# NSA's z gates and its selection and window values computed in the Strassen phase, kept in DRAM by rows, and read back by the attention; finer steps of its background work

## The chip, the cores and the metric

One core of one Trainium2 chip runs the whole kernel in one launch. The metric is the device time of one execution in microseconds (us); lower is better. The engines are named as the profile names them: PE (TensorE's matmuls), PEld (its weight loads), DVE (VectorE), ACT (ScalarE), POOL (GpSimd) and SP (SyncE, which here only issues DMAs).

## The reference, cut to what matters

One hybrid decoder layer on 512 tokens of width 2048, all in float32. FoX is an attention with a forget gate, NSA one with three branches (compressed, selected, window); each has 8 heads of 128.

```python
h = x @ w_in                       # 2048 -> 11808 columns, cut into the groups below
(fq, fk, fv, ff, fz, nq, nkc, nvc, nks, nvs, nkw, nvw, ng, nz, ga, gb) = split(h)
y_a = (fox(fq, fk, fv, ff) * silu(fz)) @ w_a
y_b = (nsa(nq, K and V of each branch, gates(ng)) * silu(nz)) @ w_b
merged = sigmoid(ga) * y_a + sigmoid(gb) * y_b
out = layer_norm(2 ** 0.25 * x + merged @ w_o)
```

The change concerns `nz` (1024 columns, one block of 128 for each NSA head) and `nvs` and `nvw` (256 columns each, one block of 128 for each of the two groups of four heads).

## The kernel before, in words

Every product is made of three matmuls (`mm3`, L105): both operands are split into a high part of 32-bit "r" type and the remainder, and high x high, high x low and low x high are summed in PSUM. A split (`split`, L96 on ACT for the high part, L97 on DVE for the low part) precedes every use of a weight or of an intermediate result.

The weights come as a stream of units. `stream` walks the list `units`; before unit n it emits the split of unit n + 3 (`AHEAD`), whose raw weights SP has loaded before. The order of every engine's instructions is the order in which this Python code emits them; nothing reorders them afterwards.

There are two ways to make columns of `h`:

- A dense projection (`proj`, `dense`) makes 128 columns for all 512 tokens, transposed: [128 columns, 512 tokens]. It has 16 tiles of the contraction with 3 matmuls of 128x512 each, in 4 units, and ends with `evac`.
- The phase of seven products (`pairs`, called by `phase_split`) makes two blocks of `width` columns by Strassen's scheme, with tokens, contraction and columns each cut in two: 7 products x 8 tiles x 2 token tiles x 3 = 336 matmuls of 128x`width` instead of 384. Some of its operands are sums of weights, made on DVE and by accumulating DMAs that POOL issues. Its results lie by rows (tokens on partitions); `keep` stores them in DRAM. Before, it makes FoX's v (L1108 into `v_d`) and most of the two merge gates (`sig_d`): three jobs of width 512 and two of width 384.

The phases follow each other: two first projections and some small ones, the phase of seven products, FoX's heads, NSA's heads, the remaining merge gates (four dense projections of 128 columns, `evac_sig`), then the output products with `w_a`, `w_b`, `w_o`, and the layer norm.

The attention itself is background work: Python generators which `tick` advances by one step. `dense` calls `tick` after every second of its tiles, so 8 times per projection. The queue `sq` runs the score half of one head at a time (`nsa_s`: scores into two banks "s" of PSUM, then in the next step the DVE instruction of L397 that adds the bias and finds the minimum, and ACT's exp of L399; a step later DVE's reciprocal and normalization, L404 and L406). The queue `tq` runs the value half (`nsa_t`: PE transposes of the probabilities, L417, into two banks "pt"; in the next step the split into `pT` on ACT and DVE; two steps later the product with the values). One call of `tick` emits, in this order, a step of every job in `active`, a step of the value half and a step of the score half. `drain` calls `tick` without matmuls of a projection in between, until a condition holds.

In the NSA phase before, the order of the projections is q0 z0, K and V of group 0 (ks, kw, vs, vw), q1 z1 q2 z2 q3 z3, K and V of group 1, q4 z4 ... q7 z7, and then the four gate tiles. `nsa_open`, ahead of the first ks, drains FoX's attention; `o_open`, ahead of the last gate tile, drains NSA's. `evac_z` (L294, L295) applies the gate function to a projection; `evac_v` copies V, transposes it on PE (L357) and splits it.

Of the kernel before, what the change touches and what calls it, by code (L numbers as in the profile page):

```python
# [20 lines left out]
P = 128  # L21
# [42 lines left out]
def layer(ctx, tc, x, w_in, b_f, pos_k, pos_v, wk1, wk2, wv1, wv2, w_a, w_b, w_o, ln_g, ln_b, rel, onehot, out):  # L64
    nc = tc.nc

    def dram(t, off, ap):
        return bass.AP(tensor=t.tensor, offset=t.offset + off, ap=ap)
# [21 lines left out]
    def bank(tag, bufs):  # L90
        return ps.tile([P, S], F32, name=tag, tag=tag, bufs=bufs)

    def split(hi, lo, src, scale=None):

        if scale is None:
            nc.scalar.activation(hi, src, AF.Copy)  # L96
            nc.vector.tensor_tensor(lo, src, hi.bitcast(F32), op=ALU.subtract)  # L97
        else:
            nc.scalar.activation(hi, src, AF.Copy, scale=scale)
            nc.vector.scalar_tensor_tensor(lo, src, scale, hi.bitcast(F32), op0=ALU.mult, op1=ALU.subtract)  # L100
# [35 lines left out]
    def drain(cond):  # L136
        for _ in range(5000):
            if cond():
                return
            tick()  # L140
        raise AssertionError("the background work stands still")
# [70 lines left out]
                u["pre"] = pre  # L212
            units.append(u)

    def dense(w, ncols, col, rows, get_src, evac, pre=None, each=None):

        kts = rows // P
        st = {}

        def pe(u, k0):  # L220
            if k0 == 0:
                st["ps"] = bank("d", 2)
            hi, lo = (t.rearrange("p (k c) -> p k c", c=P) for t in u["w"])
            for k in range(4):
                if each:
                    each(k0 + k)
                mm3(st["ps"], (hi[:, k], lo[:, k]), get_src(k0 + k), k0 + k == 0, k0 + k == kts - 1)
                if k % 2 == 1:
                    tick()
            if k0 + 4 == kts:  # L230
                evac(st["ps"])

        for k0 in range(0, kts, 8):
            add_chunk(lambda r: r.rearrange("p (k c) -> p k c", c=P),
                      dram(w, k0 * P * ncols + col, [[ncols, P], [P * ncols, 8], [1, P]]),
                      lambda u, half, k0=k0: pe(u, k0 + 4 * half), pre=pre if k0 == 0 else None)
# [4 lines left out]
    def proj(col, evac, **kw):  # L241
        dense(w_in, IN_COLS, col, D, x_src, evac, **kw)
# [12 lines left out]
    def pool(name):  # L255
        return stage[name][1]
# [9 lines left out]
    def take(tag):  # L266

        drain(lambda: free[tag] > 0)
        free[tag] -= 1

    def take_later(tag):
        while free[tag] == 0:
            yield
        free[tag] -= 1
# [4 lines left out]
    def z_tile():  # L279
        return pool("hd").tile([P, S], F32, name="z", tag="z", bufs=5)  # L280
# [8 lines left out]
    def evac_z(key):  # L289
        def f(p):  # L290
            take("z")

            zt[key] = t = z_tile()
            nc.scalar.activation(t, p, AF.Tanh, scale=0.5)  # L294
            nc.vector.scalar_tensor_tensor(t, t, 1.0, p, op0=ALU.add, op1=ALU.mult)  # L295
            done.add(("z", key))
        return f
# [16 lines left out]
    def v_load(h):  # L314
# [11 lines left out]
        split(hi, lo, v)  # L326
        done.add(("v", ("f", h)))

    def evac_q(key):
        def f(p):  # L330
            take("q")
            t = pool("attn").tile([P, 2, S], F32R, name="q", tag="q", bufs=2)
            split(t[:, 0], t[:, 1], p, SC)
            qt[key] = t
            done.add(("q", key))
        return f

    def evac_k(key, dst):
        def f(p):
            hi, lo = dst()  # L340
            split(hi, lo, p)
            done.add(("k", key))
        return f

    def evac_v(key, dst):

        def f(p):
            take("vT")
            v = pool("attn").tile([P, S], F32, name="vT", tag="vT", bufs=1)
            nc.scalar.activation(v, p, AF.Copy)  # L350

            def job():
                yield
                yield
                m = bank("m", 1)
                for j in range(NT):
                    nc.tensor.transpose(m[:, j * P:(j + 1) * P], v[:, j * P:(j + 1) * P], ident)  # L357
                free["vT"] += 1
                hi, lo = dst()
                split(hi, lo, m)  # L360
                done.add(("v", key))
                yield
            active.append(job())
        return f


# [8 lines left out]
    def wait_for(*keys):  # L375
        while not all(k in done for k in keys):
            yield
# [236 lines left out]
    zd = [dp.tile([P, S], F32, name=f"z_d{h}") for h in range(NZD)]  # L614
    rawd = {(kv, g): dp.tile([P, S], F32, name=f"raw_d{kv}{g}") for kv in "kv" for g in range(G)}
    vd = dp.tile([S, H * DH], F32, name="v_d")
    sigd = [dp.tile([S, D], F32, name=f"sig_d{g}") for g in range(2)]

    def tables():
# [274 lines left out]
    def nsa_k_dst(br, g):  # L894
        def f():
            if br == "s":
                drain(lambda: all(("s", ("n", h)) in done for h in range(g * HPG)))
                t = pool("nsa").tile([P, 2, KW], F32R, name="nk", tag="nk", bufs=1)
                kt_[g] = t
                nc.vector.tensor_copy(t[:, :, :CP], kt_["c", g].bitcast(F32))  # L900
            t = kt_[g]
            c0 = CP if br == "s" else CP + S
            return t[:, 0, c0:c0 + S], t[:, 1, c0:c0 + S]
        return f

    def nsa_v_dst(br, g):
        def f():
            assert all(("t", ("n", h)) in done for h in range(g * HPG)), "values still held"
            t = pool("nsa").tile([P, 2, NT, DH], F32R, name="nv" + br, tag="nv" + br, bufs=1)
            vt[br, g] = (t[:, 0], t[:, 1])  # L910
            return t[:, 0].rearrange("p j d -> p (j d)"), t[:, 1].rearrange("p j d -> p (j d)")
        return f

    def nsa_kv(g):
        def vpre():
            drain(lambda: all(("t", ("n", h)) in done for h in range(g * HPG)))
        proj(C_KS + g * DH, evac_k(("s", g), nsa_k_dst("s", g)), pre=None if g else nsa_open)
        proj(C_KW + g * DH, evac_k(("w", g), nsa_k_dst("w", g)))
        proj(C_VS + g * DH, evac_v(("s", g), nsa_v_dst("s", g)), pre=vpre if g else None)
        proj(C_VW + g * DH, evac_v(("w", g), nsa_v_dst("w", g)))  # L920


    HT = 2
# [159 lines left out]
    def t_op(n):  # L1083
        if n in ("T4", "T1"):
            return lambda e, k, i: left[n][:, e, k, i * P:(i + 1) * P]
        return lambda e, k, i: left[n, k // 2][:, e, k % 2, i * P:(i + 1) * P]
# [24 lines left out]
    def kept(dst, func, base_col, cols, width):  # L1111
        f = keep(dst, func)
        f.base = base_col
        return (w_in, IN_COLS, 0, [base_col + c for c in cols], width, f)
# [3 lines left out]
    def phase_split():  # L1118
        jobs = [kept(vd, AF.Copy, C_FV, (0, S), S)]
        for g, c in enumerate((C_GA, C_GB)):  # L1120
            jobs.append(kept(sigd[g], AF.Sigmoid, c, (0, S), S))
            jobs.append(kept(sigd[g], AF.Sigmoid, c, (2 * S, 2 * S + W2), W2))
        ops = {n: t_op(n) for n in ("T1", "T2", "T3", "T4")}
        ops.update({"B11": b_op(0, 0), "B21": b_op(1, 0), "B22": b_op(1, 1)})
        pairs(jobs, ops, KT // 2, pairs_open)
# [30 lines left out]
    for kv, h in (("v", 4), ("k", 1)):  # L1156
        for n, l0 in enumerate(range(0, CMP_LEN, 2 * LB)):
            units[at[h] + 4 * n + 4:at[h] + 4 * n + 4] = cmp_units(kv, l0)
    for h in range(H):
        if h % HPG == 0 and h:  # L1160
            nsa_kv(h // HPG)
        proj(C_NQ + h * DH, evac_q(("n", h)))
        proj(C_NZ + h * DH, evac_z(("n", h)))
        if h == 0:
            nsa_kv(0)


    sig, osp, fin = {}, {}, {}

    def evac_sig(g, j):  # L1170

        def f(p):
            take("z")
            t = z_tile()
            nc.scalar.activation(t, p, AF.Sigmoid)

            def job():
                yield
                yield
                m = bank("s", 2)  # L1180
                for i in range(NT):
                    nc.tensor.transpose(m[:, i * P:(i + 1) * P], t[:, i * P:(i + 1) * P], ident)
                nc.scalar.activation(t, m, AF.Copy)
                nc.sync.dma_start(dram(sigd[g][:], j * P, [[D, P], [P * D, NT], [1, P]]),
                                  t.rearrange("p (i c) -> p i c", i=NT))
                free["z"] += 1
                yield
            active.append(job())
        return f
# [12 lines left out]
                    yield  # L1202
        active.append(job())

    for j in range(NG // P, KT):
        for g, c in enumerate((C_GA, C_GB)):
            proj(c + j * P, evac_sig(g, j), pre=o_open if (j, g) == (KT - 1, 1) else None)

    BANKS = [("pt", 2), ("pt", 2), ("o", 1), ("m", 1)], [("d", 2), ("d", 2), ("s", 2), ("s", 2)]

# [351 lines left out]
```

## Time and profile before

| what | us |
|---|---|
| median of 3 runs | 1523.29 (1522.69 to 1524.36) |
| the profiled execution's own time | 1525.12 |
| its span, first to last instruction | 1523.4 |
| PE busy | 1504.0 (99% of the span) |
| DVE busy | 836.7 (55%) |
| ACT busy | 647.0 (42%) |
| phase of seven products | from 106 to about 467 |
| FoX's heads | from about 467 to 755 |
| NSA's heads and the remaining gates | from 755 to about 1156 |

The granted clock was 0.999 of the full 2.4 GHz. A PE that is busy is not one at its peak: the duration of a matmul in the trace holds its latency too, and consecutive ones overlap. The time that a matmul costs is the distance between the starts of neighbours.

### The profile page before, as it was taken

To read this page: it belongs to the slowest core of one execution; us is meant where nothing else is said; L and a number is where in the kernel's file an instruction comes from. 1 tells how busy PE (TensorE), PEld (TensorE's weight loads), DVE (VectorE), ACT (ScalarE), POOL (GpSimd) and SP (SyncE) were. 2 spreads that over 40 slices of the span, in tenths; PEclk is the share of its full clock that TensorE was granted. 3 is DMA by queue.
4 is the path that set the end of the run, shared out by engine and by line. 5 is a ranking of instruction groups with operands and counts; after the bars stand their busy time and mean duration, and the time that the engine had idled before them with its cause. 6 is when DMAs were issued, how large, how long until landed. Compare 5 with 4: busy or idle time off the path is not lost.

```text
span 1523.4 us, 19742 instructions
## 1 busy us (share of the span) xinstructions
PE 1504.0 (99%) x7161; PEld 1256.0 (82%) x7161; DVE 836.7 (55%) x1680; ACT 647.0 (42%) x1270; POOL 210.6 (14%) x351
## 2 busy tenths in 40 slices
PE   8999999999999999999999999999999999999998
PEld 6688788987998888888888888888888888888886
DVE  4566666666664654654435665366645444444455
ACT  6255656555563543533334444244444222222233
POOL 1211010111114623422000000000002010030001
PEclk9999999999999999999999999999999999999999
DMA  8678585877666443443233222322236343272236
GB/s 227 156 220 183 183 194 161 197 214 180 161 161 190 144 136 91 144 138 108 72 98 90 75 77 73 87 76 77 56 96 209 125 145 125 91 249 97 97 111 166
DMA packets 202929, 208.59 MB, mean 137 GB/s; under 512 B 12768, under 2 KB 153104, under 8 KB 202832
## 3 DMA queue, kind: packets, MB, share of 16 engines
q1 hardware_dynamic: 181936, 158.88, 34.9%
q0 software_dynamic: 20608, 47.93, 14.2%
q8 instruction: 56, 0.92, 0.2%
q10 hardware_dynamic: 288, 0.52, 0.1%
q14 instruction: 41, 0.34, 0.1%
HBM read 190.72 MB, written 20.22 MB: 138 GB/s over the span
## 4 chain that ended last, share of the span: by engine, by line
PE 92%; DVE 4%; ACT 2%; DMA 1%; issue 1%; POOL 0%; SPq 0%; ACTq 0%; DVEq 0%; POOLq 0%
PE d L105 50%; PE s L105 13%; PE pt L105 9%; PE o L105 9%; PE m L105 6%; DVE wl L97 2%; PE pt L417 2%; ACT wh L96 1%; PE m L111 1%; PE o L111 0%; PE d L1234 0%; DMA sig_d<-zo 0%; DVE c L993 0%; DVE s L992 0%; DMA vT<-v_d 0%
## 5 line engine op out<-in xcount | busy, mean ns | idle before, releaser
L105 PE MATMUL d<-big,wh 128*128 128x512 f32 x1792 | 568.7, 398 | 1.4 <-ACT wh L96 1.1
L97 DVE TENSOR_TENSOR wl<-wr,wh 128x512 fp32r<-128x512 f32 (+1 forms) x492 | 331.5, 682 | 379.1 <-ACT wh L96 368.7
L96 ACT ACTIVATE wh<-wr 128x512 fp32r<-128x512 f32 (+1 forms) x492 | 299.8, 618 | 388.5 <-PE d L105 140.0
L105 PEld LDWEIGHTS d<-big,wh 128*128 128x128 f32 x1792 | 324.1, 188 | 65.2 <-issue 2.1
L105 PE MATMUL d<-big,wl 128*128 128x512 f32 x896 | 351.5, 392 | 0.1
L105 PEld LDWEIGHTS d<-big,wl 128*128 128x128 f32 x896 | 168.5, 188 | 37.9 <-DVE wl L97 0.9
L399 ACT ACTIVATE p<-p,mn 128x128 f32<-128x128 f32 (+3 forms) x96 | 54.0, 562 | 133.5 <-DVE mn L397 133.5
L97 DVE TENSOR_TENSOR wl<-s,wh 128x512 fp32r<-128x512 f32 (+1 forms) x120 | 75.2, 637 | 54.1 <-ACT wh L96 53.9
L96 ACT ACTIVATE wh<-s 128x512 fp32r<-128x512 f32 (+1 forms) x120 | 69.0, 587 | 58.3 <-DVE wl L97 32.8
L105 PE MATMUL s<-wh,T 128*128 128x512 f32 (+1 forms) x320 | 93.2, 367 | 0.0
L105 PE MATMUL o<-wh,big 128*128 128x512 f32 (+1 forms) x224 | 84.3, 376 | 2.6 <-ACT wh L96 2.6
L105 PE MATMUL m<-wh,big 128*128 128x512 f32 (+1 forms) x224 | 83.7, 374 | 0.0
L105 PE MATMUL d<-wh,big 128*128 128x512 f32 (+1 forms) x240 | 74.4, 376 | 0.0
L97 DVE TENSOR_TENSOR pT<-pt,pT 128x512 fp32r<-128x512 f32 (+1 forms) x96 | 46.6, 488 | 44.3 <-ACT pT L96 43.9
L105 PEld LDWEIGHTS s<-wh,T 128*128 128x128 f32 x320 | 59.2, 188 | 7.5
L805 POOL TENSOR_SCALAR af<-raw,posT 128x31 f32<-128x31 f32 x128 | 65.2, 531 | 0.1
L96 ACT ACTIVATE pT<-pt 128x512 fp32r<-128x512 f32 (+1 forms) x96 | 41.2, 433 | 46.8 <-PE pt L417 46.0
L105 PE MATMUL s<-wl,T 128*128 128x512 f32 (+1 forms) x160 | 58.7, 367 | 0.0
L105 PEld LDWEIGHTS o<-wh,big 128*128 128x128 f32 x224 | 42.0, 188 | 10.6 <-ACT wh L96 4.5
L105 PEld LDWEIGHTS d<-wh,big 128*128 128x128 f32 x240 | 44.7, 188 | 7.2 <-ACT wh L96 0.4
L967 POOL DMA_DIRECT2D r<-in_w_in_dram x20 | 24.0, 1198 | 187.5 <-DVE wl L97 77.4
L489 POOL DMA_DIRECT2D bt<-skew_d x8 | 4.3, 540 | 324.9 <-DVE mn L397 257.5
(314 smaller groups left out, 2398.9 us busy)
## 6 DMA issues: line engine op xcount, KB each, us to landing
wr<-in_w_in_dram SPq DMA_DIRECT2D x147, 512.0 KB, 3.7
wr<-in_w_o_dram SPq DMA_DIRECT2D x32, 512.0 KB, 3.6
wr<-in_w_in_dram SPq DMA_DIRECT2D x24, 384.0 KB, 3.8
wr<-in_w_a_dram SPq DMA_DIRECT2D x16, 512.0 KB, 3.6
om<-sig_d POOLq DMA_DIRECT2D x32, 256.0 KB, 4.9
wr<-in_w_b_dram SPq DMA_DIRECT2D x16, 512.0 KB, 3.6
r<-in_w_in_dram SPq DMA_DIRECT2D x12, 512.0 KB, 5.3
r<-in_w_in_dram POOLq DMA_DIRECT2D x12, 512.0 KB, 10.4
```

The costliest lines, as they stand in the source:

```text
L96: nc.scalar.activation(hi, src, AF.Copy)
L97: nc.vector.tensor_tensor(lo, src, hi.bitcast(F32), op=ALU.subtract)
L105: nc.tensor.matmul(o, u, v, start=first and n == 0, stop=last and n == 2, **kw)
L111: nc.tensor.matmul(*u, start=first and u is whole, stop=last and u is whole)
L399: nc.scalar.activation(row, row, AF.Exp, bias=it["mn"][:, i:i + 1], scale=-1.0, accum_out=it["l"][:, i:i + 1])
L417: nc.tensor.transpose(b[:, (i - j) * P:(i - j + 1) * P], pt[:, OFF[i] + j * P:OFF[i] + (j + 1) * P], ident)
L489: nc.gpsimd.dma_start(bt, dram(skew_d, h * P * RL + P - 1, [[RL - 1, P], [1, S]]))
L805: nc.gpsimd.tensor_scalar(af[:, l, g], src, posT[:, po0 + ll:po0 + ll + 1], None, op0=ALU.add)
L967: nc.gpsimd.dma_start(two(n, k), rows(jobs[j], quad[0] * kh + k - 1, quad[1]), accum_op=ALU.add)
```

## The change

The columns `nz` and `nvs`/`nvw` are no longer made by 8 + 4 dense projections within the NSA phase. Two jobs join the phase of seven products: one of width 512 for `nz`, one of width 256 for the four value blocks. Their results are stored by rows in the new DRAM tensors `nz_d` and `nv_d`.

Each head's z is then loaded by POOL (`nz_load`), transposed on PE, and gated as before; each group's values are loaded by POOL (`nv_load`) and split, without a transpose. `tick` is now called after three of four tiles in the NSA phase's projections (`STEPS`), so 12 times per projection. The order of the projections is q0, one gate tile, ks0 kw0, q1 q2 q3 q4, ks1 kw1, q5 q6 q7, and three gate tiles.

```diff
-    def dense(w, ncols, col, rows, get_src, evac, pre=None, each=None):
+    def dense(w, ncols, col, rows, get_src, evac, pre=None, each=None, steps=(1, 3)):
...
-                if k % 2 == 1:
+                if k in steps:
                     tick()
...
+    def rows_of(dt, ncols, col):
+
+        return dram(dt[:], col, [[ncols, P], [P * ncols, NT], [1, DH]])
+
+    def nz_load(h):
+
+        yield from take_later("z")
+        t = z_tile()
+        nc.gpsimd.dma_start(t.rearrange("p (j d) -> p j d", d=DH), rows_of(nzd, H * DH, h * DH))
+        for _ in range(4):
+            yield
+        m = bank("m", 1)
+        for j in range(NT):
+            nc.tensor.transpose(m[:, j * P:(j + 1) * P], t[:, j * P:(j + 1) * P], ident)
+        nc.scalar.activation(t, m, AF.Tanh, scale=0.5)
+        nc.vector.scalar_tensor_tensor(t, t, 1.0, m, op0=ALU.add, op1=ALU.mult)
+        zt["n", h] = t
+        done.add(("z", ("n", h)))
+        yield
+
+    def nv_load(g):
+
+        for br, c in (("s", C_VS), ("w", C_VW)):
+            yield from take_later("vT")
+            v = pool("attn").tile([P, S], F32, name="vT", tag="vT", bufs=1)
+            nc.gpsimd.dma_start(v.rearrange("p (j d) -> p j d", d=DH),
+                                rows_of(nvd, C_VW + G * DH - C_VS, c - C_VS + g * DH))
+            yield from wait_for(*[("t", ("n", h)) for h in range(g * HPG)])
+            for _ in range(3):
+                yield
+            free["vT"] += 1
+            hi, lo = nsa_v_dst(br, g)()
+            split(hi, lo, v)
+            done.add(("v", (br, g)))
...
-    def evac_v(key, dst):
...
+    nzd = dp.tile([S, H * DH], F32, name="nz_d")
+    nvd = dp.tile([S, C_VW + G * DH - C_VS], F32, name="nv_d")
...
+    STEPS = (1, 2, 3)
+
     def nsa_kv(g):
-        def vpre():
-            drain(lambda: all(("t", ("n", h)) in done for h in range(g * HPG)))
-        proj(C_KS + g * DH, evac_k(("s", g), nsa_k_dst("s", g)), pre=None if g else nsa_open)
-        proj(C_KW + g * DH, evac_k(("w", g), nsa_k_dst("w", g)))
-        proj(C_VS + g * DH, evac_v(("s", g), nsa_v_dst("s", g)), pre=vpre if g else None)
-        proj(C_VW + g * DH, evac_v(("w", g), nsa_v_dst("w", g)))
+        proj(C_KS + g * DH, evac_k(("s", g), nsa_k_dst("s", g)), pre=None if g else nsa_open, steps=STEPS)
+        proj(C_KW + g * DH, evac_k(("w", g), nsa_k_dst("w", g)), pre=lambda: active.append(nv_load(g)), steps=STEPS)
...
+        jobs.append(kept(nzd, AF.Copy, C_NZ, (0, S), S))
+        jobs.append(kept(nvd, AF.Copy, C_VS, (0, C_VW - C_VS), G * DH))
...
-    for h in range(H):
-        if h % HPG == 0 and h:
-            nsa_kv(h // HPG)
-        proj(C_NQ + h * DH, evac_q(("n", h)))
-        proj(C_NZ + h * DH, evac_z(("n", h)))
-        if h == 0:
-            nsa_kv(0)
...
-    for j in range(NG // P, KT):
-        for g, c in enumerate((C_GA, C_GB)):
-            proj(c + j * P, evac_sig(g, j), pre=o_open if (j, g) == (KT - 1, 1) else None)
+    rest = [(j, g) for j in range(NG // P, KT) for g in range(2)]
+
+    def gate_tile(pre=None):
+        j, g = rest.pop()
+        proj((C_GA, C_GB)[g] + j * P, evac_sig(g, j), pre=pre, steps=STEPS)
+
+    for h in range(H):
+        proj(C_NQ + h * DH, evac_q(("n", h)), pre=lambda h=h: active.append(nz_load(h)), steps=STEPS)
+        if h == 0:
+            gate_tile()
+        if h % HPG == 0:
+            nsa_kv(h // HPG)
+    while rest:
+        gate_tile(pre=o_open if len(rest) == 1 else None)
```

## Rows read from the trace of the kernel before

**Rows 1.** The page's first part: busy us (share of the span) and instructions by engine.

```profile
PE 1504.0 (99%) x7161; PEld 1256.0 (82%) x7161; DVE 836.7 (55%) x1680; ACT 647.0 (42%) x1270; POOL 210.6 (14%) x351
```

**Rows 2.** Windows: stretch, then busy us per engine, clock, DMA share, GB/s.

```profile
core 0: us, PE busy (x) PEld busy (x) DVE busy (x) ACT busy (x) POOL busy (x), PEclk, DMA share, GB/s
...
755.00:1145.00 390.00, 389.31 (x1935) 327.18 (x1934) 210.15 (x572) 158.68 (x361) 4.31 (x8) 1.00 0.30 80
...
1029.00:1039.00 10.00, 10.00 (x53) 8.52 (x53) 7.29 (x25) 4.09 (x11) 0.00 (x0) 1.00 0.21 54
```

**Rows 3.** Timeline, PE, a dense projection alone: start, us, engine, line, operation.

```profile
786.00 0.62 PE L105 MATMUL d<-big,wh 128*128 128x512 f32 x2
...
786.68 0.62 PE L105 MATMUL d<-big,wh 128*128 128x512 f32 x2
```

**Rows 4.** Timeline, PE, the phase of seven products: first matmuls of three products.

```profile
261.90 0.33 PE L105 MATMUL pt<-wh,T 128*128 128x384 f32 x1
...
270.25 0.33 PE L105 MATMUL d<-wh,T 128*128 128x384 f32 x1
...
399.96 0.33 PE L105 MATMUL pt<-wh,T 128*128 128x384 f32 x1
```

**Rows 5.** Timeline, PE, matmuls of width 256 and four transposes, each with its successor.

```profile
757.98 0.51 PE L105 MATMUL s<-k,q 128*128 128x256 f32 x3
758.32 0.63 PE L105 MATMUL d<-big,wh 128*128 128x512 f32 x2
...
769.15 0.60 PE L417 MATMUL pt<-ident,p 128*128 128x128 f32 x4
769.51 0.72 PE L105 MATMUL d<-big,wh 128*128 128x512 f32 x2
```

**Rows 6.** Timeline, head 0's scores alone: first and last matmul (PE) and read (DVE).

```profile
805.04 0.60 PE L105 MATMUL s<-nk,q 128*128 128x320 f32 x3
...
806.38 0.28 DVE L397 CUSTOM_DVE_ANT_0 p<-s,bt 128x128 f32<-128x128 f32 x1
...
817.97 0.85 PE L105 MATMUL s<-nk,q 128*128 128x512 f32 x3
...
821.46 0.68 DVE L397 CUSTOM_DVE_ANT_0 p<-s,bt 128x512 f32<-128x512 f32 x1
```

**Rows 7.** Timeline, ACT and DVE, while score and value steps run together.

```profile
1024.81 0.49 ACT L96 ACTIVATE pT<-pt 128x384 fp32r<-128x384 f32 x1
...
1025.33 0.56 DVE L97 TENSOR_TENSOR pT<-pt,pT 128x384 fp32r<-128x384 f32 x1 [1.26 <-ACT pT L96]
...
1026.81 0.41 DVE L397 CUSTOM_DVE_ANT_0 p<-s,bt 128x256 f32<-128x256 f32 x1
...
1027.27 0.51 ACT L399 ACTIVATE p<-p,mn 128x256 f32<-128x256 f32 x1 [1.97 <-DVE mn L397]
...
1027.78 0.61 ACT L96 ACTIVATE wh<-wr 128x512 fp32r<-128x512 f32 x1
...
1029.03 0.42 DVE L97 TENSOR_TENSOR pT<-pt,pT 128x256 fp32r<-128x256 f32 x1
...
1029.98 0.55 DVE L397 CUSTOM_DVE_ANT_0 p<-s,bt 128x384 f32<-128x384 f32 x1
```

**Rows 8.** The page's groups: splits; busy us, mean ns of one, idle before.

```profile
L97 DVE TENSOR_TENSOR wl<-wr,wh 128x512 fp32r<-128x512 f32 (+1 forms) x492 | 331.5, 682 | 379.1 <-ACT wh L96 368.7
...
L97 DVE TENSOR_TENSOR pT<-pt,pT 128x512 fp32r<-128x512 f32 (+1 forms) x96 | 46.6, 488 | 44.3 <-ACT pT L96 43.9
...
L96 ACT ACTIVATE pT<-pt 128x512 fp32r<-128x512 f32 (+1 forms) x96 | 41.2, 433 | 46.8 <-PE pt L417 46.0
```

**Rows 9.** Timeline, PE: transposes of a gate tile right after a drain.

```profile
1144.72 0.66 PE L1182 MATMUL s<-ident,z 128*128 128x128 f32 x4 [0.69 <-ACT z L1175]
```

**Rows 10.** Groups by line, 805 to 1145: the table load ahead of the sigmoid.

```profile
L1175 ACT ACT_TABLE_LOAD x1 | 1.3, 1283 | 0.0
```

**Rows 11.** DMA issues: KB each, median us to landing.

```profile
vT<-v_d POOLq DMA_DIRECT2D x8, 256.0 KB, 4.1
```

More of the change, by code (lines that the diff above doesn't have):

```diff
@@ L342, in f @@
             done.add(("k", key))
-        return f
-    def evac_v(key, dst):
[L347 to L363, printed above, removed]
         return f
```

## The prediction, made before the changed kernel ran

> **What bounds the kernel now.** I read the page's first part, then the windows by phase, then the timeline of PE alone, to see what one matmul really costs, and last the timeline of ACT and DVE in the NSA phase, which tells how near they are to being the limit there. PE is busy 99% of the span [rows 1] and in the NSA phase all but 0.7 of 390 us, at full clock (the windows' 1.00) [rows 2]. So before the change a PE microsecond removed is a microsecond won, as long as DVE and ACT keep up; DVE is busy 210 of those 390 us, but 7.29 of 10 us where score and value steps run together [rows 2].
>
> Prices on PE. In a dense projection three 512-wide matmuls start every 0.68 us [rows 3]: 0.2267 us each, 48 x 0.2267 = 10.88 us for a projection of 128 columns. At width 384, one product's 48 matmuls take 270.25 - 261.90 = 8.35 us, 0.174 each; one job of width 384 and one of 512 together take 399.96 - 261.90 = 138.06 us with all their stalls [rows 4]. Three matmuls of width 256 take 0.34 us (0.113 each), four transposes 0.36 us (0.09 each) until their successor starts [rows 5].
>
> **What moves to the seven products.** Twelve projections go: eight of z, 8 x 10.88 = 87.0 us, four of V, 43.5 us. The z job is one of width 512: its share of the 138.06 us is 0.2267/(0.2267 + 0.174), 78.1 us. Gain 8.9 us. The V job is 336 matmuls of width 256. The lines through 512 and 384 and on to 256 give 0.121, three in a row 0.113: 38.0 to 40.7 us. The pair of jobs lost 138.06 - 336 x 0.4007 = 3.4 us to stalls, 1.7 per job. Narrow units are worse covered: three units of lead are 2.2 us instead of 4.1, against a split whose instructions shrink less than in proportion. So I add 1.7 to 4 us and take 43 us. Gain 0.5 us (from 5.5 gained, without a stall, to 1.2 lost).
>
> **What is added on PE.** z needs 32 transposes, V no longer needs its 16: 16 more at 0.09 to 0.11, 1.6 us. One gate tile now stands right before the drain of `nsa_open`; its transposes wait for their sigmoid, as those ahead of `o_open` do: 0.69 us idle [rows 9] and 0.15 us to restart, so 0.85 us; if the table load of 1.28 us [rows 10] is not done in advance, 2.1 us. The sigmoid now comes at two places with exps between, which makes two more such loads; ACT has room for them elsewhere (41% busy in this phase [rows 2]). The Trainium skill, in "ScalarE: Activation LUTs", section "What ACT_TABLE_LOAD costs", speaks against this order: it counts a drain with each switch, 2.66 us in all. The trace has the load at 1.28 us [rows 10]; by the page the sum would be at most 1.4 us larger.
>
> nz's transposes are on PE's queue and wait for a DMA issued four steps earlier. The nearest load, of the same shape, lands in 4.1 us [rows 11]; four steps are 3.6 us of projection (a step's share is 10.88/12 = 0.907) and about as much attention. Only head 0, with little attention beside it, may wait: 0.5 us. POOL has 4.3 us of work in this phase [rows 2], so nothing holds the load up there. The new stores go to SP, two DMA issues per output pair as in the five jobs before; nobody waits for them until NSA. `drain` ahead of the second group's V goes: PE did not idle there, so nothing is won.
>
> **Do the steps suffice?** A head's scores take 12 calls of `tick`, its values 13. Before, a head had two projections, 16 calls; now one projection, 12 calls. From the end of kw0 to `o_open` stand 11 projections, 132 calls; the chain of value halves needs 12 + 8 x 13 = 116 and stands about 20 for the second group's K. So the last head ends some four steps into the drain of `o_open`, where the gate tile's sigmoid is awaited anyway: nothing. The work fits, but each step is now shorter, and that is the problem.
>
> **Can ACT and DVE follow?** Within a step the code sets a loop on two in-order engines: ACT splits the transposes (high), DVE makes the low part, then normalizes the row before, then reads the scores, ACT takes the exp; only then comes ACT's next high part. Rows 7 show one turn: high part at 1024.81, low part at 1025.33, read at 1026.81, exp at 1027.27, ACT free for the next thing at 1027.78: 2.97 us. The next read comes at 1029.98, 3.17 us after the one before, with a weight's split in between [rows 7]. PE's own steps there are two tiles of projection, 1.36 us, and by the prices below about 1.2 us of attention: 2.5 us. It did not stall, since by the count of steps the values of a head run some five steps ahead of the next head's scores, and only three or four steps hold the whole loop.
>
> After the change they overlap all along: six pairs (values of h with scores of h + 1, twice three), of 13 steps, of which 8 hold both reads and splits. PE's time for these 8: projection 8 x 0.907 = 7.3; scores 8 x 0.49 = 3.9 (head 0 alone made 7 steps in 817.97 - 805.04 = 12.93 us [rows 6], 1.85 each, less 1.36 of projection); transposes, value products and z's transposes at the prices above 5.6. Sum 16.8 us. The loop's time for the same 8: head 0's eight reads alone ran 806.38 to 821.46 [rows 6], 2.15 per step, 17.2 for eight, less the weight splits that are now rarer (one in three steps instead of one in two: 1.33 fewer at 0.61 + 0.68 [rows 7, 8]) 15.5; plus eight high and low parts at 0.433 + 0.488 [rows 8], 7.4. Sum 22.9 us, 6.1 more than PE.
>
> How much of 6.1 PE feels depends on how far it may run ahead. Two score banks and two transpose banks: step k's scores wait for the read of k - 2. That is two steps of 2.1 us, less what the read itself takes (high part to read's end, 2.4 us) where it was not overlapped: 1.8 to 4.2 us. So 1.9 to 4.3 us of stall per pair; in the five light steps that follow, PE has 6 us and the loop some 4, so the lag is worked off and nothing accumulates. Going through one pair step by step with these durations I get a stall near 2; I take 2.5, six times: 15. The scores of heads 0 and 4 alone: loop 15.5, PE 8 x 1.40 = 11.2, 4.3 short, of which the banks take 1.4 to 2.8; 2 us each: 4. Sum 19 us. Bounds: nothing (PE has not idled on this loop in the trace), and all of the shortage, 6 x 6.1 + 2 x 4.3 = 45 us.
>
> **The sum.** -8.9 - 0.5 + 1.6 + 0.85 + 0.5 + 19 = +12.5 us. The profiled execution took 1525.12, 1.8 above the median 1523.29; the sum against it is 1537.6, against the median 1535.8. I predict 1535.
>
> **Rivals.**
> 1. *PE stays the bound* (other side: faster). The banks and the light steps absorb the loop's lag. Speaks for it: no idle PE in NSA before, DVE with 12 x 4 splits fewer (33 us) needs 177 us of the phase's new 260, 68%. Against: shares say nothing of a loop across two engines. Then the sum is without its 19: -6.5, 1517. It decides at 6.5 us of stall, 0.8 per overlapped or single head of the eight. The Trainium skill, "Perfetto Trace Analysis", section "Identifying the Most-Contended Engine", takes this side: it names the engine of highest occupancy as the one to serve, and PE's stays above DVE's. Here the trace agrees so far: at 73% of DVE [rows 2] PE did not wait.
> 2. *The loop binds in full*: the lag is not worked off between pairs. +38.5 us, 1562. For it: in rows 7 the loop has no slack of its own. Against: the second group's K (24 steps without attention) empties the queue once.
> 3. *The gain and the stall cancel*: 3.5 to 9.5 us of stall, within 3 us of before.
> That the change would not do what it says is ruled out by the count of matmuls: 576 of width 512 are replaced by 336 of 512 and 336 of 256.
>
> **Numbers.** Forecast (stall 10 to 35 us) 0.54, its own range 1526 to 1551; rival 1 0.24; rival 3 0.12; rival 2 0.10. What measurement can tell is about 0.2%, 3 us. Faster 0.24, same 0.12, slower 0.64. Range 1514 to 1550: most of rival 1, all of rival 3, the forecast; beyond it lie most of rival 2 and what a V job without stalls adds to rival 1.
>
> **What would show it.** The two new jobs at 78 and 43 us between first matmuls of their T4 products. In the NSA phase, idle PE ended by DVE's reads (L397) or low parts (`pT`) in steps where value and score steps run together, some 2 to 3 us per head, DVE near 80% there. If PE's gaps there sum to under 6 us, rival 1 holds. A wait at the transposes of nz for the load, or at the new jobs' splits for `wr`, above 1 us each would show costs that I put at nothing.

## The result, and the profile after

The changed kernel takes 1543.7 us (median of 4 runs, 1543.4 to 1545.1), the kernel before 1523.6 in the same session: ratio 1.0134, 95% interval 1.0117 to 1.0152. It is slower by 20.1 us. 1535 was forecast; the measured time is 8.7 us above that and within the range of 1514 to 1550. The profiled execution took 1543.83 us, its span is 1542.1.

The page's first line after, to set against [rows 1]: PE is as long busy as before within 2 us, although by the sum it has some 7 us less to do, and its share fell from 99 to 97%. No other engine comes near it.

```profile
PE 1502.7 (97%) x7273; PEld 1252.7 (81%) x7273; DVE 885.2 (57%) x1776; ACT 684.4 (44%) x1364; POOL 239.6 (16%) x379
```

Where in the span PE's time went is read from its timeline, at the first matmul of each part: the z job, the V job, FoX's first dense projection, q0, and the first product with `w_a`.

```profile
459.08 0.39 PE L105 MATMUL pt<-wh,T 128*128 128x512 f32 x1
...
536.96 0.28 PE L105 MATMUL pt<-wh,T 128*128 128x256 f32 x1
...
563.14 0.38 PE L105 MATMUL o<-wh,big 128*128 128x256 f32 x1 [0.83 <-ACT wh L96]
...
566.66 0.38 PE L105 MATMUL o<-wh,big 128*128 128x256 f32 x1 [0.77 <-ACT wh L96]
...
581.26 0.73 PE L105 MATMUL d<-big,wh 128*128 128x512 f32 x2 [0.27 <-ACT zo L1121]
...
873.13 0.61 PE L105 MATMUL d<-big,wh 128*128 128x512 f32 x2
...
903.36 0.66 PE L1190 MATMUL s<-ident,z 128*128 128x128 f32 x4 [0.69 <-ACT z L1183]
...
1174.92 0.39 PE L105 MATMUL pt<-wh,osp 128*128 128x512 f32 x1
```

The z job took 536.96 - 459.08 = 77.9 us, the V job 581.26 - 536.96 = 44.3, with two waits of some 0.8 us for its own splits. The NSA stage, from q0 to `w_a`, took 1174.92 - 873.13 = 301.8 us; before, the same stretch ran from 752.9 to 1156.1, 403.2 us (PE's timeline of the kernel before):

```profile
752.94 0.62 PE L105 MATMUL d<-big,wh 128*128 128x512 f32 x2
...
1156.12 0.39 PE L105 MATMUL pt<-wh,osp 128*128 128x512 f32 x1
```

Twelve projections at 10.88 us less, the transposes and the gate tile's 0.85 us (here again 0.69 idle, as in [rows 9], then the restart) make 403.2 - 130.6 + 1.6 + 0.85 = 275.1. So 26.7 us of the stage are accounted for by no work: lost time. They are larger than the whole loss.

The windows after, the stage and about one pair (scores of one head with values of the one before), answer to [rows 2]. PE was idle 18 of 302 us, where it had been idle 0.7 of 390; no other engine is near full in the pair, DVE at 73% stands highest.

```profile
core 0: us, PE busy (x) PEld busy (x) DVE busy (x) ACT busy (x) POOL busy (x), PEclk, DMA share, GB/s
...
873.00:1175.00 302.00, 283.98 (x1437) 232.30 (x1436) 188.49 (x542) 136.77 (x333) 17.49 (x29) 0.99 0.28 79
943.00:968.00 25.00, 23.49 (x125) 19.06 (x125) 18.30 (x58) 11.45 (x32) 1.29 (x2) 1.00 0.22 64
```

Idle PE time here is less than the 26.7 us lost, in part because a matmul that restarts after a wait has a longer record (0.48 us for three 32-wide ones below, of which the next matmul starts after 0.33) and counts as busy. The lost time is better read from starts.

What PE waits for is in the timeline of all engines during the pair of heads 1 and 2. This is one turn of the loop that [rows 7] show for the kernel before.

```profile
977.79 0.41 DVE L411 CUSTOM_DVE_ANT_0 p<-s,bt 128x256 f32<-128x256 f32 x1
...
978.25 0.51 ACT L413 ACTIVATE p<-p,mn 128x256 f32<-128x256 f32 x1 [2.22 <-DVE mn L411]
978.36 0.48 PE L105 MATMUL s<-nk,q 128*128 128x32 f32 x3 [0.73 <-DVE mn L411]
...
978.76 0.58 ACT L343 ACTIVATE z<-m 128x512 f32<-128x512 f32 x1
...
979.24 0.48 ACT L96 ACTIVATE pT<-pt 128x384 fp32r<-128x384 f32 x1
979.37 0.69 DVE L344 SCALAR_TENSOR_TENSOR z<-z,m 128x512 f32<-128x512 f32 x1 [1.15 <-ACT z L343]
...
979.97 0.55 DVE L97 TENSOR_TENSOR pT<-pt,pT 128x384 fp32r<-128x384 f32 x1
980.44 0.15 DVE L418 RECIPROCAL r<-l 128x1 f32<-128x1 f32 x1
980.63 0.41 DVE L420 TENSOR_SCALAR p<-p,r,gates 128x256 f32<-128x256 f32 x1
980.67 0.30 PE L431 MATMUL pt<-ident,p 128*128 128x128 f32 x1 [0.34 <-DVE r L418]
...
981.06 0.55 DVE L411 CUSTOM_DVE_ANT_0 p<-s,bt 128x384 f32<-128x384 f32 x1
...
981.65 0.62 ACT L413 ACTIVATE p<-p,mn 128x384 f32<-128x384 f32 x1 [1.93 <-DVE mn L411]
981.76 0.93 PE L105 MATMUL s<-nk,q 128*128 128x512 f32 x3 [0.79 <-DVE mn L411]
```

Read it as a ring. DVE's read of the scores (977.79) gives the minimum; ACT, idle for 2.22 us until then, takes the exp (978.25). In ACT's order z's gate function and the next high part stand behind that exp (978.76, 979.24). In DVE's order z's second half stands first; DVE sits idle 1.15 us for it, then makes the low part (979.97), then the reciprocal and the normalization of the row just exponentiated (980.44, 980.63), and only then the next read (981.06). One turn is 981.06 - 977.79 = 3.27 us. For most of it one of the two engines waits for the other, and both times PE's next scores wait for the minimum, 0.73 and 0.79 us, as the two score banks are unread. Of the 18.0 us that PE is idle in the stage, 9.7 end with such a read. No engine is full; the ring is.

Grouped over 900 to 1175 us, the idle time ahead of each link says the same (busy us, mean ns | idle us just before, its releaser):

```profile
L413 ACT ACTIVATE p<-p,mn 128x128 f32<-128x128 f32 (+3 forms) x64 | 35.9, 561 | 101.7 <-DVE mn L411 101.7
...
L97 DVE TENSOR_TENSOR wl<-wr,wh 128x512 fp32r<-128x512 f32 x57 | 39.2, 688 | 35.0 <-ACT wh L96 34.0
L97 DVE TENSOR_TENSOR pT<-pt,pT 128x512 fp32r<-128x512 f32 (+1 forms) x64 | 31.3, 488 | 33.8 <-ACT pT L96 33.8
...
L418 DVE RECIPROCAL r<-l 128x1 f32<-128x1 f32 x64 | 10.0, 156 | 7.2 <-ACT p L413 7.1
...
L344 DVE SCALAR_TENSOR_TENSOR z<-z,m 128x512 f32<-128x512 f32 x7 | 4.8, 687 | 8.1 <-ACT z L343 8.1
```

### The profile page after: what moved, and what is told of

It reads as the page before. It is cut to its first block, busy times and chain, and to the rows that moved or that the text cites. A ratio compares the mean times of both kernels' runs of the same rounds, so it can differ in the third digit from the quotient of the medians.

```text
span 1542.1 us, 20376 instructions
## 1 busy us (share of the span) xinstructions
PE 1502.7 (97%) x7273; PEld 1252.7 (81%) x7273; DVE 885.2 (57%) x1776; ACT 684.4 (44%) x1364; POOL 239.6 (16%) x379
## 4 chain that ended last, share of the span: by engine, by line
PE 81%; DVE 9%; ACT 5%; issue 3%; DMA 1%; POOL 0%; ACTq 0%; SPq 0%; POOLq 0%; DVEq 0%
PE d L105 38%; PE s L105 13%; PE pt L105 10%; PE o L105 9%; PE m L105 6%; DVE wl L97 3%; ACT wh L96 2%; DVE p L411 1%; PE pt L431 1%; ACT p L413 1%; DVE p L420 1%; DVE pT L97 1%; PE m L111 1%; DMA wr<-in_w_in_dram 1%; PE o L111 0%
## 5 line engine op out<-in xcount | busy, mean ns | idle before, releaser
L97 DVE TENSOR_TENSOR wl<-wr,wh 128x512 fp32r<-128x512 f32 (+2 forms) x492 | 324.0, 668 | 336.3 <-ACT wh L96 327.0
L96 ACT ACTIVATE wh<-wr 128x512 fp32r<-128x512 f32 (+2 forms) x492 | 294.7, 608 | 374.9 <-PE d L105 111.8
L105 PE MATMUL d<-big,wh 128*128 128x512 f32 x1408 | 448.1, 399 | 1.2 <-ACT wh L96 0.4
L97 DVE TENSOR_TENSOR wl<-s,wh 128x512 fp32r<-128x512 f32 (+2 forms) x168 | 101.5, 615 | 72.0 <-ACT wh L96 71.7
L96 ACT ACTIVATE wh<-s 128x512 fp32r<-128x512 f32 (+2 forms) x168 | 93.5, 568 | 77.4 <-DVE wl L97 43.6
L105 PE MATMUL s<-wh,T 128*128 128x512 f32 (+2 forms) x448 | 125.1, 358 | 0.0
L105 PE MATMUL o<-wh,big 128*128 128x512 f32 (+2 forms) x288 | 105.5, 368 | 4.7 <-ACT wh L96 4.7
L105 PE MATMUL m<-wh,big 128*128 128x512 f32 (+2 forms) x288 | 104.5, 365 | 0.0
L105 PE MATMUL d<-wh,big 128*128 128x512 f32 (+2 forms) x304 | 90.6, 368 | 0.2 <-ACT wh L96 0.2
L105 PE MATMUL s<-wl,T 128*128 128x512 f32 (+2 forms) x224 | 80.2, 358 | 0.0
```

The costliest lines, as they stand in the source:

```text
L105: nc.tensor.matmul(o, u, v, start=first and n == 0, stop=last and n == 2, **kw)
```

## The experiments

T1 in the expectations is the prediction's theory, that the loop of ACT and DVE holds PE up; the other theories say in each expectation what they hold. All times are medians beside the kernel before on the same chip (1524.1 to 1524.7). Differences between variants are differences of these medians; the kernel before itself moved by about 0.5 us from the first result (1523.6) to most of them. Where an expectation counts some 9 us lost in the stage of the kernel before, it does not show the working; PE's idle time there is 0.7 us of 403.2.

### Which half of the change costs: V alone, z alone

`v_only` keeps the V job and leaves z dense, with the order and the two calls of `tick` of the kernel before; `z_only` keeps the z job and the changed order and steps, and makes V dense behind K.

```
v_only:  - jobs.append(kept(nzd, AF.Copy, C_NZ, (0, S), S))
         + proj(C_NZ + h * DH, evac_z(("n", h)))        # behind each q
         STEPS = (1, 3)
z_only:  - jobs.append(kept(nvd, AF.Copy, C_VS, (0, C_VW - C_VS), G * DH))
         + proj(C_VS + g * DH, evac_v(...)); proj(C_VW + g * DH, evac_v(...))
```

> Only the V job moves to the seven products; z stays dense, in the order and with the steps of before (16 steps of background work per head). Theory 1 (the stall is the loop between ACT and DVE, which binds once a head has only 12 steps): no new stall in the NSA phase, so before's 1523.6 minus 43.5 for four projections, plus 44.3 for the V job, minus 1.6 for 16 transposes: 1523, 1520 to 1526. Theory 2 (the loss comes with reading values back by rows, or with the narrow job): at least a third of the loss, 1530 or more.

> Only the z job moves; V stays dense behind the K projections, all with the finer steps. Theory 1: heads still have 12 steps, but V's projections part values and scores of the first head of each group, so four overlapped pairs instead of six: stall about 18 instead of 27; -87.0 + 77.9 + 3.2 for 32 transposes + 0.9 for the gate tile ahead of the drain + 18 is +13, 1537, 1531 to 1542. Theory 2 (loss from V's part): 1520 or less.

V alone: 1523.4 us, ratio 0.9993 (0.9984 to 1.0002). z alone: 1544.7, ratio 1.0135 (1.0118 to 1.0152). So V's move is worth nothing either way, as the sum had it, and the whole loss is with z's. That z alone is no better than both, although V's projections are back as cover, was not expected (1531 to 1542). Its trace has the four overlapped pairs that were expected, and PE is idle 6.6 us in their projections. But where a head's scores run alone, PE is idle 5.8 us in four projections more, and 1.7 in the two where values run alone: parting the pairs mostly moved the waits.

### Are the finer steps to blame?

```
- STEPS = (1, 2, 3)
+ STEPS = (1, 3)
```

> The changed kernel with the steps of before, 8 per projection instead of 12. Theory 1: the cause is the number of projections left as cover, not the fineness of the steps. 88 steps stand before the last drain where about 136 are needed, so some 48 steps run without a projection, each at a turn of the loop (about 2.9 us, 1.2 of it matmuls of the attention): some 80 us more idle PE, of which the 20 or so of stall inside the projections are given back: 1600, 1575 to 1620. Theory 3 (the finer steps themselves do the harm): back to 1525 or less.

1543.0 us, ratio 1.0122 (1.0107 to 1.0137): both expectations missed. The windows say why: in two heads' projections PE now hardly waits, and the same time is lost at the end, where the remaining steps run in `o_open`'s drain with no projection beside them.

```profile
951.00:1005.00 54.00, 53.92 (x289) 45.78 (x288) 39.03 (x122) 25.50 (x68) 2.61 (x4) 1.00 0.29 79
1127.00:1174.00 47.00, 36.62 (x192) 30.40 (x191) 28.72 (x76) 24.54 (x53) 3.65 (x7) 0.93 0.16 50
```

In this kernel the fineness of the steps decided where the wait is, hardly how long it is (the stage takes 299.7 us instead of 301.8). My 1600 for the coarse steps counted many more uncovered steps than came about.

### Opening a link: the low part of pT later

The low part goes to the end of the step, behind the read of the scores; same instructions, another place in DVE's order.

```
 def split_p(it):
-    split(t[:, 0, :n], t[:, 1, :n], it.pop("b")[:, :n])
+    nc.scalar.activation(t[:, 0, :n], b[:, :n], AF.Copy)
+    late.append(lambda: nc.vector.tensor_tensor(t[:, 1, :n], b[:, :n], t[:, 0, :n].bitcast(F32), op=ALU.subtract))
 def tick():
     ...
+    while late: late.popleft()()
```

> The changed kernel; in each step DVE makes the low part of the probabilities last, after it has normalized and read the scores, so that ACT's high part runs beside that and ACT's exp beside the low part. No work is added or left out. Theory 1: a full turn of the loop falls from 2.9 us to about 2, near PE's own step; most of the 27 us of stall goes: 1525, 1519 to 1531. Theory 4 (DVE's or PE's total work binds, not the order): DVE has the same work, so no change, 1542 to 1545.

1535.4 us, ratio 1.0074 (1.0059 to 1.0089): 8.3 of the 26.7 us come back: neither the 1519 to 1531 of T1 nor the unchanged time of T4. The read now still stands behind the normalization, which waits for the exp, and the transposes wait for their bank until the later low part has read it (timeline of PE in this run):

```profile
958.24 0.63 PE L433 MATMUL pt<-ident,p 128*128 128x128 f32 x4 [0.57 <-DVE pT L441]
...
981.34 0.30 PE L433 MATMUL pt<-ident,p 128*128 128x128 f32 x1 [0.67 <-DVE pT L441]
```

DVE was 85% busy in 943 to 968 in this run, which raised a second theory (T5): that its load itself is the limit. The next four tell that apart.

### DVE's load, or the order of the links?

`norm_act` and `norm_pool` take the normalization's multiplication off DVE; `lo_norm_late` leaves it there, but a step later; `lo_late_before` makes the later low part in the kernel before.

```
norm_act:       - nc.vector.tensor_scalar(row, row, r, it["gate"], op0=ALU.mult, op1=ALU.mult)
                + nc.vector.tensor_tensor(r, r, it["gate"], op=ALU.mult)
                + nc.scalar.activation(row, row, AF.Copy, scale=r)
norm_pool:      + nc.gpsimd.tensor_scalar(row, row, r, it["gate"], op0=ALU.mult, op1=ALU.mult)
lo_norm_late:   lo_late, and
                - staged(steps, (mm, red, norm))
                + staged(steps, (mm, red, None, norm))
lo_late_before: the kernel before with the edit of lo_late
```

> The changed kernel, but in NSA's heads the 128-row multiplication of norm_row goes from VectorE to ScalarE (a copy with scale r; r takes the gate in a 128x1 multiplication before). In the stretch 943:968 it cost VectorE 0.47 us x 8 of its 18.3 us. T1 (the loop of NSA's heads is limited by what stands in line on VectorE between two rows' minima): VectorE's share of a pair falls by some 8 x (0.47 - 0.16) = 2.5 us, as much as a pair was late (25 against 21.8): 1524 to 1530 us. T4 (what counts is the length of the chain score, minimum, exponential, transposition, copies, whoever does it): the same number of links, ScalarE now carries 11.5 + 4.5 of 25 us: 1540 to 1546 us.

> The changed kernel, but in NSA's heads the 128-row multiplication of norm_row goes from VectorE to GpSimd, which is idle there (1.3 of 25 us). T1: VectorE is relieved by 8 x 0.47 = 3.8 us a pair, and ScalarE carries nothing more, so 1520 to 1528 us, a little under the variant with ScalarE, unless GpSimd needs so long for a row (no row of this shape in the trace; over 2 us) that it sets the pace itself: then 1545 to 1570. T4: no change, 1541 to 1546.

> The changed kernel with the low part of pT at the end of a step, as in the run that gave 1535.4 us, and the normalization one step later, so that it need not wait for the exponential of its own step's neighbour. VectorE's load is the same. T1 in the form 'VectorE's order': another few us come back, 1528 to 1533. T5 (VectorE's load itself, 85 per cent busy in the dense stretch, is now the limit, and its order is spent): 1533 to 1537, or slightly worse, since a head takes one step more.

> Control: the kernel before with the same later low part of pT. There TensorE is busy nearly without a gap in NSA's heads (9 us lost in the whole stage), so all theories expect no change: 1522 to 1525 us, ratio 0.998 to 1.002. If it gains over 4 us, the low part's place matters without the loop, and its 8 us in the changed kernel say nothing of the loop.

Measured: on ScalarE 1547.9 us, ratio 1.0156 (1.0139 to 1.0173), worse than the changed kernel by 4.2 (3.6 when each is set against its own kernel before) and above both expectations; on GpSimd 1539.2, ratio 1.0098 (1.0083 to 1.0113), between the two expectations; later on DVE 1528.9, ratio 1.0030 (1.0017 to 1.0043); the control 1523.8, ratio 0.9998 (0.9989 to 1.0008).

DVE's load fell from 18.3 to 15.5 of 25 us (943 to 968) with ScalarE's help, and the kernel became slower; so T1 in the form of DVE's load is out; ACT, at 15.6 of 25 us with the multiplication, was not full either. The groups of that run show where it went: the multiplication waits on ACT for DVE's reciprocal, 51.7 us in all, and the next high parts and exps stand behind it. So the multiplication became one link more in the ring.

```profile
L421 ACT ACTIVATE p<-p,r 128x128 f32<-128x128 f32 (+3 forms) x64 | 35.2, 561 | 51.7 <-DVE r L420 36.0 <-DVE r L418 9.8 <-DVE tc L533 5.9
```

The same work a step later, when its exp has long been done, brought 6.5 us more than the later low part alone, with DVE busier than in the changed kernel (19.7 of 25 us). The gain of 4.5 us with GpSimd fits both readings by itself: its 0.65 us a row take a link off DVE's order as well as load.

### All links opened

`norm_late` is the later normalization alone. `lnzw_late` opens four: low part, normalization, z's second half a step after its first, and in NSA's phase the low part of a weight at the end of a step. `lnzw_late_pool` has GpSimd's multiplication besides. `lnw_late_before` opens in the kernel before the three links that exist there.

```
norm_late:  + staged(steps, (mm, red, None, norm))
lnzw_late:  lo_norm_late, and
  def nz_load(h):
      nc.scalar.activation(t, m, AF.Tanh, scale=0.5)
  +   yield
      nc.vector.scalar_tensor_tensor(t, t, 1.0, m, op0=ALU.add, op1=ALU.mult)
  def split_w(n):
  +   if "nsa" in stage and "chunk" in u and not any(k in u for k in ("into", "prep", "after", "late")):
  +       nc.scalar.activation(hi, src, AF.Copy)
  +       def low(u=u, hi=hi, lo=lo, src=src):
  +           nc.vector.tensor_tensor(lo, src, hi.bitcast(F32), op=ALU.subtract)
  +           load(u["chunk"] + 2 + u["half"])
  +       late.append(low)
  +       continue
```

> The changed kernel with the normalization of NSA's rows one step later, and nothing else (the low part of pT stays beside its high part). T6 (the time goes into a ring of waits: minimum on VectorE, exponential on ScalarE, then in the two engines' orders high part on ScalarE, low part and normalization on VectorE, next minimum; each link that is opened gives its part back whatever the engines carry): the later low part gave 8 us and both together 15, so this alone gives 5 to 9: 1535 to 1539. T5 (VectorE's load): the same work, one step more a head: no change, 1542 to 1546.

> Low part of pT at the end of a step, normalization a step later (together 1528.9 us), and two links more of the same kind: z's VectorE half a step after its tanh on ScalarE (VectorE sat 1.15 to 1.79 us before it), and in NSA's phase the low part of a weight at the end of a step (VectorE sat some 0.6 to 1.3 us before it). T6: TensorE still lost 21.7 us in NSA's stage, against 9.1 in the kernel before; about half of the difference goes: 1520 to 1525, no slower than the kernel before. T5 (VectorE carries 19.7 of 25 us and is the limit itself): 1527 to 1530.

> The same four links opened, and the normalization's multiplication on GpSimd as well (0.69 us a row there), which takes 3.8 of 25 us from VectorE. T6 with little load left: 1515 to 1521, faster than the kernel before by up to the 8.9 us that z's product saves less the 1.6 us of transpositions. T5: this is the one that gains, 5 us or more under the run without GpSimd. If GpSimd's length hurts the chain it is no better than without: 1521 to 1526.

> Second control: the kernel before with the later low part of pT, the normalization one step later, and the later low part of a weight in NSA's phase (z's step does not exist there; z comes out of its own projection). T6 (the ring of waits costs only where TensorE has too little of its own to do meanwhile; before had 12 projections more): nothing to win in the stage that loses 9 us in all, 1520.5 to 1525, and the 1519 us of the changed kernel with these links opened is the product of z at last paying. Rival: the four links are worth some 5 us in any kernel: 1517 to 1520, and then the change itself pays nothing even with the links opened.

Measured: the later normalization alone 1537.9 us, ratio 1.0091 (1.0076 to 1.0106); four links 1519.1, ratio 0.9971 (0.9958 to 0.9984); with GpSimd 1518.8, ratio 0.9962 (0.9948 to 0.9976); the kernel before with its three links 1524.7 beside 1524.7, ratio 0.9997 (0.9987 to 1.0006).

The links add up: 8.3 us for the low part, 5.8 for the normalization, 14.9 for both, 9.8 more for z's half and the weights' low parts (these two were not run apart). In all 24.6 of the 26.7 us; some 2 us of such a sum can be clock, as the last section shows. Four links give a kernel faster than the changed one and, by some 5 us (0.3%), than the one before. In the kernel before, the three of these edits that exist there give nothing: PE has a second projection in each head and the ring turns behind it. GpSimd's relief on top gives nothing either, which settles T5. The windows of the two runs, four links and four links with GpSimd, show PE full with DVE at 19.71 and at 15.74 of 25 us (in the 25 us after these, PE is busy 24.35 and 24.66):

```profile
943.00:968.00 25.00, 25.00 (x142) 21.64 (x141) 19.71 (x64) 12.67 (x34) 1.35 (x2) 1.00 0.31 85
```

```profile
943.00:968.00 25.00, 25.00 (x143) 21.55 (x142) 15.74 (x52) 13.28 (x34) 6.42 (x10) 1.00 0.36 105
```

In the run with four links the stage goes from 873.34 to 1149.64 on PE's timeline, 276.3 us: 1.2 above the 275.1 worked out without a wait.

```profile
873.34 0.39 PE L105 MATMUL d<-big,wh 128*128 128x512 f32 x1
...
1149.64 0.39 PE L105 MATMUL pt<-wh,osp 128*128 128x512 f32 x1
```

The groups of that run answer to those of the changed kernel, line for line. The instructions are as many and as long; the idle time ahead of the exp fell from 101.7 to 36.6 us, ahead of the low part from 33.8 to 17.1, of the reciprocal from 7.2 to 0.8, of z's half from 8.1 to 1.5, all over the same heads. And the read (L422) now waits for PE, 4.0 us, which it never did before.

```profile
L424 ACT ACTIVATE p<-p,mn 128x128 f32<-128x128 f32 (+3 forms) x64 | 35.8, 561 | 36.6 <-DVE mn L422 36.4
...
L450 DVE TENSOR_TENSOR pT<-pt,pT 128x512 fp32r<-128x512 f32 (+1 forms) x64 | 31.1, 487 | 17.1 <-ACT pT L449 17.0
L422 DVE CUSTOM_DVE_ANT_0 p<-s,bt 128x128 f32<-128x128 f32 (+3 forms) x64 | 30.4, 484 | 4.1 <-PE s L105 4.0
L429 DVE RECIPROCAL r<-l 128x1 f32<-128x1 f32 x64 | 9.9, 154 | 0.8 <-ACT p L424 0.8
...
L355 DVE SCALAR_TENSOR_TENSOR z<-z,m 128x512 f32<-128x512 f32 x7 | 4.8, 681 | 1.5 <-ACT z L353 1.5
```

## Why the prediction was right, point by point

- **The z job**, 78.1 us: measured 77.9. **The V job**, 43 us: measured 44.3, so it loses 0.8 us where 0.5 was to be won; its two waits for splits are the narrow units' poorer cover that the prediction named. V alone came out as no change.
- **Transposes and gate tile**, 1.6 + 0.85 us: the wait of 0.69 us and the restart came as put. What the sum missed is that the like wait ahead of `o_open` [rows 9] is gone in the trace after, so the gate tile cost next to nothing and the 275.1 us may be up to 0.85 too high. The second table load did not show on PE: it starts at 900.42 on ACT, takes 1.28 us and is done 1.01 us before the sigmoid's input. So the 1.4 us that the Trainium skill would have added by "ScalarE: Activation LUTs", section "What ACT_TABLE_LOAD costs", were not seen here; at the other load of that kind the sigmoid starts 1.29 us after the load does (1146.28 and 1144.99), with no drain in the trace.
- **The wait for nz's load**, 0.5 us: none. The trace after has PE's 32 transposes of z with no idle time ahead of them. The loads landed in 4.5 us (median of 8).

```profile
L342 PE MATMUL m<-ident,z 128*128 128x128 f32 x32 | 4.8, 272 | 0.0
```

```profile
z<-nz_d POOLq DMA_DIRECT2D x8, 256.0 KB, 4.5
```

- **The loop of ACT and DVE**, 19 us: the mechanism is the one predicted, and the runs that open its links without taking any work away show it. Its size was too small: 26.7 us by the stage's sum, 24.6 given back by opening it. The loop's time for the eight steps of a pair, put at 22.9 us, was about right: by the prediction's own measure, first read to last, a pair's eight reads take 19.3 to 20.5 us in the six pairs, 19.9 in the mean; over seven distances that is 2.84 a step, 22.7 for eight. (The turn of 3.27 us above, with z in it, is one of the longer ones.) Two errors cancel in that, which is luck. A head alone was put at 15.5 us for eight reads and takes 18.0 (15.72 for the seven distances): z's second half, which the change brings into the loop (`nz_load` runs inside `tick`, `evac_z` ran outside), stands there too, with 1.15 us of waiting and 0.69 of work (at 933.39). The high and low parts then add 4.7 us to it and not 7.4.
- The term that was mis-sized is **what PE feels of that shortage**, put at 2.5 us a pair and 2 for a head alone, the two banks and the light steps being trusted with the rest. From the start of one projection to the start of the next, on PE's timeline, the changed kernel and the one with four links open take (with the links open some work falls a step later, so sums of rows tell more than single ones):

| projection | what runs beside it | changed, us | links open, us | difference |
|---|---|---|---|---|
| q1 | scores of head 0 alone | 17.8 | 15.4 | 2.4 |
| q2, q3, q4 | pairs of heads | 25.0, 25.3, 26.1 | 21.9, 22.4, 22.2 | 3.1, 2.9, 3.9 |
| q5 | scores of head 4 alone | 19.3 | 16.8 | 2.5 |
| q6, q7, gate tile | pairs of heads | 24.8, 25.1, 26.2 | 21.9, 22.4, 21.2 | 2.9, 2.7, 5.0 |

- So the six pairs lose 20.5 us where 15 were forecast (1.7 of the last 5.0 are clock, see the last section), and the **heads alone** 4.9 where 4 were. Another 1.5 us went in q0's projection, which was in no term; the rest of the stage gives 1.4 back, 25.5 in all. How much of the ring's cost comes from PE's lost projections and how much from z's instructions in the loop is not measured: z's half was opened together with the weights' low parts.
- **Rival 1**, PE stays the bound at 1517 us, was the right price for the kernel without the ring: 1519 when the links are open. Its ground, that DVE at some 70% leaves room, was true and beside the point. The rule of the Trainium skill in "Perfetto Trace Analysis", section "Identifying the Most-Contended Engine", would have one serve PE, the fullest (it judges TensorE by its weight loads, here busy 19.06 of 25 us against DVE's 18.30); the trace after differs, with PE waiting for an engine that is 73% busy.
- **Rival 2**, the loop in full at 1562, did not come: its price was all of the shortage, 45 us of stall (38.5 net of what the change saves); 26.7 were found.
- What was to be seen in the profile was seen: waits for the minimum, and a few for the low part, where score and value steps overlap, 26.7 / 8 = 3.3 us a head for the 2 to 3 forecast. DVE near 80% was a little high: 73%.

## What to carry to other kernels

When work is taken off the engine that is full, look at what turned behind it: a loop over two in-order engines may be slower than what is left, though neither engine is near full. Price such a loop by one whole turn, from a read to the next read, with every instruction that stands in line between, those that the change moves into it too; do not trust a few buffers with most of what the loop is short by (of 6.1 us a pair PE was to feel 2.5 and felt 3.4); and open it by reordering (an instruction that waits for the other engine goes behind the one that others wait for, or a step later) before moving work to a third engine, which can add a link. In the kernel before, where the full engine still covers the loop, the same reordering was worth nothing.

## What the runs showed of the hardware that was not expected

The granted clock fell once within the stage of the changed kernel, right behind short waits. In the last pair PE waited 0.25 and 0.74 us within 2 us; from 1131 us on the granted clock was at half, its 1.2 GHz level, though PE was busy throughout, and it came back some 3.4 us later. The windows of 1 us and PE's timeline there:

```profile
1130.00:1131.00 1.00, 0.26 (x2) 0.21 (x2) 0.67 (x4) 0.30 (x1) 0.00 (x0) 1.00 0.00 0
1131.00:1132.00 1.00, 1.00 (x4) 0.77 (x4) 0.18 (x1) 1.00 (x4) 0.00 (x0) 0.55 0.07 16
1132.00:1133.00 1.00, 1.00 (x4) 0.81 (x3) 0.96 (x5) 0.58 (x2) 0.00 (x0) 0.50 0.00 0
...
1134.00:1135.00 1.00, 1.00 (x5) 0.73 (x5) 0.97 (x4) 0.36 (x1) 0.00 (x0) 0.74 0.29 28
1135.00:1136.00 1.00, 1.00 (x8) 0.87 (x7) 0.22 (x2) 0.87 (x4) 0.00 (x0) 1.00 0.91 226
```

```profile
1129.63 0.44 PE L431 MATMUL pt<-ident,p 128*128 128x128 f32 x2 [0.25 <-DVE pT L97]
1130.82 1.36 PE L105 MATMUL s<-nk,q 128*128 128x512 f32 x3 [0.74 <-DVE mn L411]
1131.98 1.05 PE L105 MATMUL d<-big,wh 128*128 128x512 f32 x2
1132.83 0.63 PE L105 MATMUL d<-big,wl 128*128 128x512 f32 x1
1133.26 1.05 PE L105 MATMUL d<-big,wh 128*128 128x512 f32 x2
```

Three 512-wide matmuls that start every 0.68 us at full clock [rows 3] took 1133.26 - 1131.98 = 1.28 us. Over the 3.4 us that is some 1.7 us lost, part of the 26.7 and in no term of the prediction.

What brings the clock down is not shown. Like waits, 2.8 us in all, stand in q4's projection, and there the clock stayed at 1.00. Of the profiled variants, those with the low part later, alone and with the later normalization, have two such stretches in their stage, the later normalization alone one, the four links none, and the slowest of all, with the multiplication on ScalarE, none either, though PE is idle 19.3 us in its stage. A difference of one or two microseconds between variants can therefore be clock.

GpSimd took 0.65 us for a row of 128 to 512 columns (mean of 64), against 0.45 on DVE and 0.56 on ScalarE.
